# Two-layer backbone on one core: expert weights split 2,048 wide, strided reads in place of strided writes, and mixing's even rows in plain fp32

## The chip, the cores and the metric

The kernel runs on one core of a Trainium2 chip. The metric is the device time of one execution in microseconds (us). Five engines work side by side, each through its own instructions in a fixed order: TensorE (PE; its weight loads are PEld), VectorE (DVE), ScalarE (ACT), GpSimd (POOL) and SyncE (SP), which here only issues DMAs. An instruction waits for what it reads, and a write waits until the buffer's last readers are done. TensorE writes into PSUM, and the others read it from there.

## The reference

Two layers over 1,024 tokens of width 1,024, all in fp32. Layer 0 mixes tokens by grouped-query attention, layer 1 by a 2-D Fourier transform in four channel groups followed by a linear map. After each comes a mixture of 32 experts in four groups: top-1 group, then the top two experts in it.

```python
for i in range(DEPTH):                       # DEPTH = 2
    ...
    h = _modulate(x, norm_mix[i], sh1, sc1)  # RMS norm * (1 + scale) + shift
    y = _gqa_attention(...) if kind == 0 else _fourier_mix(h, fourier_w_o[j])
    x = x + g1 * y
    x = x + g2 * _hier_moe(_modulate(x, norm_ffn[i], sh2, sc2), *moe_p)
return _rms_norm(x, final_norm)

def _fourier_mix(h, w_o):
    hg = h.reshape(b, n, FOURIER_GROUPS, d // FOURIER_GROUPS)
    f = jnp.fft.fft2(hg, axes=(1, 3), norm='ortho').real
    return f.reshape(b, n, d) @ w_o

def expert_block(args):                      # per expert: D 1,024, width 512
    xblk, e = args
    return (jax.nn.silu(xblk @ w1[e]) * (xblk @ w3[e])) @ w2[e]
```

## The kernel before

**Products.** A large fp32 product is three products in fp32r, TensorE's faster reading of fp32: each operand is the sum of a high part (a copy rounded to fp32r, by ScalarE) and a low part (the operand minus its high part, mostly by VectorE). mm3 (L207 to L209) multiplies high by high, low weights by high, high by low. wh and wl are the parts of a weight, xh and xl those of an expert's transposed input, gh and gl those of its transposed hidden rows.

**Experts.** phase_moe runs 32 experts on up to 104 gathered rows each. Weights come from memory in 1 MB pieces of 128 by 2,048, two each for w1, w3 and w2. In the order of use they are w1 of expert e, w2 of expert e−1, w3 of e. `quarter` (L1245) takes 1,024 columns of a piece, copies them into wh (L1249) and subtracts into wl (L1254); of every twelfth quarter GpSimd subtracts. There are five pairs of buffers (NSP), and `get` splits three quarters ahead of use (AHEAD). The first five low parts of a layer (NLATE) are put off until after the first gather (`finish_late`, L1264). The next piece is loaded when a raw buffer becomes free (`feed`, L1240). Some pieces lie as a list of two tiles of 1,024.

For expert e the program's order is: w1's first half into h1; gT of expert e−1, four transposes of its hidden rows (L1358), then gh on ScalarE (L1361) and gl on VectorE (L1362); w1's second half; xin of expert e+1, eight transposes of its gathered rows (L1329), then xh (L1330) and xl (L1331); the products with w2 into py; w3 into h3, with `store` of expert e−1 between (y, L1371, and a scatter-add by GpSimd, L1372); `hidden`, which is silu (L1347) and gg = silu(h1) × h3 (L1350). A scheduler then sets each engine's order from its own estimate of times. gT and xin share the PSUM tile pt, one bank of 2 KB per partition, with two buffers. The rows of an expert and their gates come from one-hot products (slot_index: L1202 on VectorE, L1205 on TensorE), four experts at a time.

**Columns.** w1 and w3 lie in memory so that the product's columns come in another order than w2's rows. gg therefore reads its inputs in order and writes at steps of 512 bytes. In the router, `route_half` (L981) does the same for the input of the logits, which route_transpose (L996, L1009) then transposes.

**Routing.** `route_part(g, m, t0, t1)` (L1093 to L1160) turns the logits of a range of 128-token tiles into chosen experts, slots and gates by many small VectorE operations. In layer 1 ROUTE_F cuts the eight tiles in 0 to 4, 4 to 6 and 6 to 8.

**Mixing.** In layer 1 `combine` scales the rows (u, L1724), folds columns c and 256−c into a sum and a difference (L1693), adds rows i and i+512 with their norms into ef (even) and subtracts them for the odd ones (L1743, L1762). `parts` splits ef into eh and el (L1700, L1701) and multiplies both by a table in high and low parts (U and UE). From the second pair on, GpSimd does a part of u, the difference folds and a running sum S of ef. `transform` then splits U (L1815) and goes on, `project` writes the mixed rows.

Of the kernel before, what the change touches and what calls it, by code (L numbers as in the profile page):

```python
# [56 lines left out]
ROUTE_F = ((0, 4), (4, 6), (6, 8))  # L57
# [4 lines left out]
AHEAD = 3  # L62
NSP = 5
NSP_EARLY = 3
# [3 lines left out]
NLATE, POOL_LAST = 5, 380  # L68
# [23 lines left out]
def host_tables():  # L92
# [28 lines left out]
    for k, v in (("pc", pc), ("ps", ps), ("cc", cc), ("cs", cs)):  # L121
        r[f"dft_{k}h"], r[f"dft_{k}l"] = two_parts(v)
# [822 lines left out]
def route_setup(g, mo, one, wk):  # L945
# [9 lines left out]
    r.gain = lambda: nc.vector.scalar_tensor_tensor(r.A2, r.A2, 1.0, nf, OP.add, OP.mult)  # L955
# [236 lines left out]
def slot_index(g, m, wk, pp, n, posm, val, tag):  # L1192
# [4 lines left out]
    for e in range(n):  # L1197
        oh = wk.tile([P, NT, CAP], BF, name="oneh", bufs=3)
# [16 lines left out]
class Moe:  # L1215
# [28 lines left out]
    def quarter(self, t, i):  # L1244

        nc = self.g.nc
        t = t[i] if isinstance(t, list) else t[:, i * 1024:(i + 1) * 1024]
        h, l = (self.hp.tile([P, 1024], F32R, name=n) for n in ("wh", "wl"))
        nc.scalar.copy(h, t)  # L1249
        if self.ns < NLATE:  # L1250
            self.late.append((l, t, h))
            return h, l
        pool = self.ns > 11 and self.ns % 12 == 9 and (self.ns < POOL_LAST or not self.l)
        i = (nc.gpsimd if pool else nc.vector).tensor_sub(l, t, h)  # L1254
        if pool:
            self.sub = i.ins
        else:
            self.vsub = i.ins
        return h, l

    def finish_late(self):

        for l, t, h in self.late:
            self.vsub = self.g.nc.vector.tensor_sub(l, t, h).ins  # L1264
# [37 lines left out]
    def get(self, n):  # L1302
        self.split(n + AHEAD)
        return self.sp.pop(n)
# [833 lines left out]
```

## Time and profile before

| | us |
|---|---|
| median of 3 runs | 2320.17 |
| lowest and highest | 2315.22, 2320.39 |
| the profiled execution | 2314.98 |
| its span in the trace | 2313.2 |

| engine | busy us | share of the span | instructions |
|---|---|---|---|
| PE | 2107.3 | 91% | 10250 |
| DVE | 1935.2 | 84% | 2822 |
| ACT | 1339.3 | 58% | 1741 |
| POOL | 1070.3 | 46% | 560 |

The span runs from the first to the last instruction; the execution has some 2 us around it. The granted clock of TensorE is 0.957 of full speed on average. In a row of the trace the first number is the start or a total in us; "out<-in" names the tiles; an arrow in brackets tells how long the engine was idle before and what ended that. Matmuls follow each other closer than their own durations, so their rate is read from the distance of starts.

### The profile page before, as it was taken

To read this page: it belongs to the slowest core of one execution; us is meant where nothing else is said; L and a number is where in the kernel's file an instruction comes from. 1 tells how busy PE (TensorE), PEld (TensorE's weight loads), DVE (VectorE), ACT (ScalarE), POOL (GpSimd) and SP (SyncE) were. 2 spreads that over 40 slices of the span, in tenths; PEclk is the share of its full clock that TensorE was granted. 3 is DMA by queue.
4 is the path that set the end of the run, shared out by engine and by line. 5 is a ranking of instruction groups with operands and counts; after the bars stand their busy time and mean duration, and the time that the engine had idled before them with its cause. 6 is when DMAs were issued, how large, how long until landed. Compare 5 with 4: busy or idle time off the path is not lost. (4 is left out here: it accounts for less than half of the span.)

```text
span 2313.2 us, 29541 instructions
## 1 busy us (share of the span) xinstructions
PE 2107.3 (91%) x10250; PEld 1436.2 (62%) x10250; DVE 1935.2 (84%) x2822; ACT 1339.3 (58%) x1741; POOL 1070.3 (46%) x560
## 2 busy tenths in 40 slices
PE   6899899999999869999999999589699999999993
PEld 3677444545446647677776776357476777777662
DVE  4878566666668789999999999666899999999995
ACT  4743444444443237677776777343487777776774
POOL 2322677777777623344334443533233444434433
PEclk8999899999999879999999999789799999999997
DMA  8544534534335779999999999644699989999996
GB/s 305 187 157 150 175 119 135 197 119 133 115 113 189 260 262 318 356 371 314 369 353 336 377 363 339 231 179 168 237 335 350 375 299 368 359 352 342 357 352 204
DMA packets 152630, 614.21 MB, mean 266 GB/s; under 512 B 26961, under 2 KB 43993, under 8 KB 106461
## 3 DMA queue, kind: packets, MB, share of 16 engines
q1 hardware_dynamic: 110188, 546.87, 64.0%
q0 software_dynamic: 24672, 54.40, 9.4%
q10 hardware_dynamic: 17616, 11.01, 1.5%
q8 instruction: 82, 1.34, 0.2%
q14 instruction: 72, 0.58, 0.1%
HBM read 559.57 MB, written 78.44 MB: 276 GB/s over the span
## 5 line engine op out<-in xcount | busy, mean ns | idle before, releaser
L208 PE MATMUL h<-wl,xh 128*104 128x512 f32 x1024 | 410.5, 401 | 18.1 <-DVE wl L1254 18.1
L207 PE MATMUL h<-wh,xh 128*104 128x512 f32 x1024 | 409.8, 400 | 0.0
L209 PE MATMUL h<-wh,xl 128*104 128x512 f32 x1024 | 406.0, 396 | 0.0
L563 DVE TENSOR_REDUCE m<-sm 128x1 f32<-128x512 f32 x360 | 201.8, 593 | 107.6 <-PE sm L562 107.1
L1318 POOL DMA_INDIRECT xg<-H,idx x64 | 116.3, 1818 | 281.4 <-PE pt L1329 126.0
L208 PEld LDWEIGHTS h<-wl,xh 128*104 128x104 f32 x1024 | 173.5, 169 | 89.4 <-DVE wl L1254 29.7
L1372 POOL DMA_INDIRECT Xs<-y,idx x64 | 192.5, 3007 | 76.3 <-DVE y L1371 47.7
L1249 ACT CAST wh<-raw 128x1024 fp32r<-128x1024 f32 x196 | 200.3, 1056 | 33.9 <-PE h L209 21.0
L1254 DVE TENSOR_TENSOR wl<-raw,wh 128x1024 fp32r<-128x1024 f32 x175 | 211.9, 1251 | 6.4 <-ACT wh L1249 6.3
L1254 DVE TENSOR_TENSOR wl<-wl,wh 128x1024 fp32r<-128x1024 f32 x163 | 211.9, 1328 | 1.8 <-ACT wh L1249 1.8
L207 PEld LDWEIGHTS h<-wh,xh 128*104 128x104 f32 x1024 | 173.5, 169 | 60.9 <-ACT xh L1330 0.5
L209 PEld LDWEIGHTS h<-wh,xl 128*104 128x104 f32 x1024 | 173.5, 169 | 60.0
L1254 DVE TENSOR_TENSOR wl<-wh 128x1024 fp32r<-128x1024 f32 x157 | 208.4, 1350 | 2.7 <-ACT wh L1249 2.3
L1249 ACT CAST wh<-wh 128x1024 fp32r<-128x1024 f32 x180 | 186.2, 1054 | 38.5 <-PE h L209 27.2
L208 PE MATMUL py<-wl,gh 128*104 128x512 f32 x512 | 203.9, 399 | 0.2 <-DVE wl L1254 0.2
L209 PE MATMUL py<-wh,gl 128*104 128x512 f32 x512 | 200.9, 394 | 0.3 <-DVE gl L1362 0.3
L1249 ACT CAST wh<-wl 128x1024 fp32r<-128x1024 f32 x172 | 178.3, 1054 | 35.5 <-PE h L209 26.5
L207 PE MATMUL py<-wh,gh 128*104 128x512 f32 x512 | 196.8, 403 | 2.0 <-ACT gh L1361 1.8
L1249 ACT CAST wh<-X 128x1024 fp32r<-128x1024 f32 x124 | 129.6, 1053 | 52.1 <-PE h L209 41.4
L1254 DVE TENSOR_TENSOR wl<-X,wh 128x1024 fp32r<-128x1024 f32 x113 | 141.3, 1282 | 3.9 <-ACT wh L1249 3.8
L1254 POOL TENSOR_TENSOR wl<-wh 128x1024 fp32r<-128x1024 f32 x23 | 68.5, 2977 | 158.7 <-issue 98.9
L562 PE MATMUL sm<-KS,qs 128*128 128x512 f32 x360 | 135.5, 383 | 0.0
(584 smaller groups left out, 4778.7 us busy)
## 6 DMA issues: line engine op xcount, KB each, us to landing
raw<-in_moe_w_dram SPq DMA_DIRECT2D x98, 1024.0 KB
wh<-in_moe_w_dram SPq DMA_DIRECT2D x90, 1024.0 KB
wl<-in_moe_w_dram SPq DMA_DIRECT2D x86, 1024.0 KB
qs<-in_moe_w_dram SPq DMA_DIRECT2D x96, 512.0 KB
raw<-in_w_mod_dram SPq DMA_DIRECT2D x43, 1024.0 KB
X<-in_moe_w_dram SPq DMA_DIRECT2D x37, 1024.0 KB
X<-in_moe_w_dram SPq DMA_DIRECT2D x50, 512.0 KB
QS<-qst ACTq DMA_DIRECT2D x32, 256.0 KB
```

Source lines behind the costliest of these rows:

```text
L207: nc.tensor.matmul(out, lh, wh, start=start, stop=False)
L208: nc.tensor.matmul(out, lh, wl, start=False, stop=False)
L209: nc.tensor.matmul(out, ll, wh, start=False, stop=stop)
L562: nc.tensor.matmul(ps[:, :kn], qs[:, h, qt * P:(qt + 1) * P], g.KS[:, g4, k0:k0 + kn], start=True, stop=True)
L563: nc.vector.reduce_max(m3[:, h, qt, b:b + 1], ps[:, :kn], axis=AX.X)
L1249: nc.scalar.copy(h, t)
L1254: i = (nc.gpsimd if pool else nc.vector).tensor_sub(l, t, h)
L1318: self.last = self.g.nc.gpsimd.indirect_dma_start(out=xg, out_offset=None, in_=self.H if src is None else src, in_offset=bass.IndirectOffs ...
L1372: return y, lambda: nc.gpsimd.indirect_dma_start(out=self.X, out_offset=bass.IndirectOffsetOnAxis(ap=idx, axis=0), in_=y, in_offset=None, ...
```

## The change

Five edits go together. (1) A whole piece (2,048 columns) is split by one copy and one subtraction, in three pairs of buffers; `get` hands out halves of it and splits two pieces ahead of use; three low parts are put off in place of five. Of every sixth piece VectorE does the first 1,024 columns and GpSimd the others. List pieces still take two operations each. (2) pt is one tile of two banks with one buffer, so xin makes xh and xl by one operation each, and gT and xin use the same tile in turn; py is one tile of two banks and y one operation. (3) silu and gg read at steps of 8 bytes in PSUM and write in order; route_half reads at 16-byte steps and writes in order, and `gain` reorders its factor once, by a ScalarE copy. (4) In layer 1 the last two route parts become one, at the end. (5) In combine ef goes into plain fp32 products with one table, without eh, el and S, and VectorE does u and all folds; ScalarE does the two-column copies.

```diff
-ROUTE_F = ((0, 4), (4, 6), (6, 8))
+ROUTE_F = ((0, 4), (4, 8))
 
 
 IB = 4
 GA = 3
-AHEAD = 3
-NSP = 5
-NSP_EARLY = 3
+NSP = 3
+NSP_EARLY = 2
 NRAW = (2, 3)
 NHELD = 11
 DROP1, DROP2 = (10, (3, 4)), (27, 2)
-NLATE, POOL_LAST = 5, 380
+NLATE, POOL_LAST = 3, 190
...
-    for k, v in (("pc", pc), ("ps", ps), ("cc", cc), ("cs", cs)):
+    r["dft_pc"] = pc
...
     nc.gpsimd.tensor_copy(by_weights(r.B2), b2.rearrange("t (q p j) -> t q p j", q=2, j=4))
-    r.gain = lambda: nc.vector.scalar_tensor_tensor(r.A2, r.A2, 1.0, nf, OP.add, OP.mult)
+
+    def gain():
+        nc.vector.scalar_tensor_tensor(nf, r.A2, 1.0, nf, OP.add, OP.mult)
+        nc.scalar.copy(r.A2.rearrange("t (q j p) -> t q j p", q=2, j=4), nf.rearrange("t (q p j) -> t q j p", q=2, j=4))
+
+    r.gain = gain
...
     ns = slice(n * 512, n * 512 + 512)
-    x, a2 = (v[:, ns].rearrange("t (p j) -> t p j", j=4) for v in (x1, r.A2))
-    g.nc.vector.tensor_mul(by_weights(r.u[t])[:, n], x, a2)
+    u, a2 = (v[:, ns].rearrange("t (j p) -> t j p", j=4) for v in (r.u[t], r.A2))
+    g.nc.vector.tensor_mul(u, x1[:, ns].rearrange("t (p j) -> t j p", j=4), a2)
...
-        oh = wk.tile([P, NT, CAP], BF, name="oneh", bufs=3)
+        if e == 2 and n == 3:
+            oh = wk.tile([P, DE], F32, name="gg", bufs=1).bitcast(BF)[:, :NT * CAP].rearrange("p (t c) -> p t c", t=NT)
+        else:
+            oh = wk.tile([P, NT, CAP], BF, name="oneh")
...
-        while self.nl < min((self.ns - len(self.late)) // 2 + self.nraw, self.limit):
+        while self.nl < min(self.ns - len(self.late) + self.nraw, self.limit):
             self.raw[self.nl] = self.load(*self.order[self.nl], eng)
             self.nl += 1
 
-    def quarter(self, t, i):
+    def half(self, t, ns=None):
 
         nc = self.g.nc
-        t = t[i] if isinstance(t, list) else t[:, i * 1024:(i + 1) * 1024]
-        h, l = (self.hp.tile([P, 1024], F32R, name=n) for n in ("wh", "wl"))
-        nc.scalar.copy(h, t)
-        if self.ns < NLATE:
-            self.late.append((l, t, h))
-            return h, l
-        pool = self.ns > 11 and self.ns % 12 == 9 and (self.ns < POOL_LAST or not self.l)
-        i = (nc.gpsimd if pool else nc.vector).tensor_sub(l, t, h)
-        if pool:
-            self.sub = i.ins
+        h, l = (self.hp.tile([P, 2048], F32R, name=n) for n in ("wh", "wl"))
+        pool = ns is not None and ns > 5 and ns % 6 == 4 and (ns < POOL_LAST or not self.l)
+        if isinstance(t, list):
+            todo = [(l[:, c:c + 1024], v, h[:, c:c + 1024], pool and c) for c, v in zip((0, 1024), t)]
+        elif pool:
+            nc.scalar.copy(h, t)
+            todo = [(v[0], v[1], v[2], c) for c in (0, 1024) for v in [[u[:, c:c + 1024] for u in (l, t, h)]]]
         else:
-            self.vsub = i.ins
+            todo = [(l, t, h, 0)]
+        if isinstance(t, list) or not pool:
+            for v in todo:
+                nc.scalar.copy(v[2], v[1])
+        if ns is not None and ns < NLATE:
+            self.late.append(todo)
+        else:
+            self.rest(todo)
         return h, l
 
+    def rest(self, todo):
+        for l, t, h, pool in todo:
+            i = (self.g.nc.gpsimd if pool else self.g.nc.vector).tensor_sub(l, t, h).ins
+            if pool:
+                self.sub = i
+            else:
+                self.vsub = i
...
+    @staticmethod
+    def quarter(t, j):
+        return [v[:, 1024 * j:1024 * j + 1024] for v in t]
...
 
     def split(self, n):
 
-        while self.ns <= min(n, 2 * len(self.order) - 1):
-            i, j = divmod(self.ns, 2)
-            self.sp[self.ns] = self.quarter(self.raw[i], j)
-            if j:
-                del self.raw[i]
+        while self.ns <= min(n, len(self.order) - 1):
+            self.sp[self.ns] = self.half(self.raw.pop(self.ns), self.ns)
             self.ns += 1
             self.feed()
 
     def get(self, n):
-        self.split(n + AHEAD)
-        return self.sp.pop(n)
+
+        i, j = divmod(n, 2)
+        self.split(i + NSP - 1)
+        return self.quarter(self.sp.pop(i) if j else self.sp[i], j)
...
         xl = self.wk.tile([P, KD, CAP], F32R, name="xl")
+        pt = self.ps.tile([P, 2, 512], F32, name="pt")
         for q in range(2):
-            pt = self.ps.tile([P, 4, CAP], F32, name="pt", bufs=2)
             for j in range(4):
-                nc.tensor.transpose(pt[:, j], xg[:, (4 * q + j) * P:(4 * q + j + 1) * P], g.ident[:CAP, :CAP])
-            nc.scalar.copy(xh[:, 4 * q:4 * q + 4], pt)
-            nc.vector.tensor_sub(xl[:, 4 * q:4 * q + 4], pt, xh[:, 4 * q:4 * q + 4])
+                nc.tensor.transpose(pt[:, q, j * CAP:j * CAP + CAP], xg[:, (4 * q + j) * P:(4 * q + j + 1) * P], g.ident[:CAP, :CAP])
+        pt = pt[:, :, :4 * CAP]
+        hv, lv = (t.rearrange("p (q j) n -> p q (j n)", q=2) for t in (xh, xl))
+        nc.scalar.copy(hv, pt)
+        nc.vector.tensor_sub(lv, pt, hv)
         return xh, xl
 
...
     def hidden(self, h1, h3):
         nc = self.g.nc
         s_ = self.wk.tile([CAP, DE], F32, name="s", bufs=1)
-        nc.scalar.activation(s_, h1, AF.Silu)
+
+        h1, h3 = (h.rearrange("t (i p j) -> t i j p", i=2, j=2) for h in (h1, h3))
+        sv = s_.rearrange("t (i j p) -> t i j p", i=2, j=2)
+        nc.scalar.activation(sv, h1, AF.Silu)
         gg = self.wk.tile([P, DE], F32, name="gg", bufs=1)[:CAP]
-
-        nc.vector.tensor_mul(gg.rearrange("t (i j p) -> t i p j", i=2, j=2), s_.rearrange("t (i p j) -> t i p j", i=2, j=2),
-                             h3.rearrange("t (i p j) -> t i p j", i=2, j=2))
+        nc.vector.tensor_mul(gg.rearrange("t (i j p) -> t i j p", i=2, j=2), sv, h3)
...
     def gT(self, gg):
         nc = self.g.nc
-        pt = self.ps.tile([P, 4, CAP], F32, name="pt", bufs=2)
+        pt = self.ps.tile([P, 2, 512], F32, name="pt")[:, 0, :4 * CAP].rearrange("p (j n) -> p j n", j=4)
         for j in range(4):
...
         y = self.wk.tile([CAP, D], F32, name="y")
-        for n in range(2):
-            ns = slice(n * 512, (n + 1) * 512)
-            nc.vector.scalar_tensor_tensor(y[:, ns], py[n], gate, self.G2[:CAP, ns], OP.mult, OP.mult)
+        nc.vector.scalar_tensor_tensor(y, py.rearrange("t n c -> t (n c)"), gate, self.G2[:CAP], OP.mult, OP.mult)
...
-                py = [mo.psum("py", 2) for n in range(2)]
+                py = mo.ps.tile([CAP, 2, 512], F32, name="py")
                 for i in range(4):
                     p = mo.get(k + i)
                     for n in range(2):
-                        mo.mm(py[n], gT, p, i, n, 1)
+                        mo.mm(py[:, n], gT, p, i, n, 1)
...
-            def fold(eng, dst, src, op):
+            def fold(dst, src, op, copy):
                 v = src.rearrange("p (g c) -> p g c", g=4)
-                g.last_fold = eng.tensor_tensor(dst[:, :, 1:128], v[:, :, 1:128], v[:, :, 255:128:-1], op).ins
+                g.last_fold = nc.vector.tensor_tensor(dst[:, :, 1:128], v[:, :, 1:128], v[:, :, 255:128:-1], op).ins
                 if op == OP.add:
-                    eng.tensor_copy(dst[:, :, 0:129:128], v[:, :, 0:129:128])
+                    copy(dst[:, :, 0:129:128], v[:, :, 0:129:128])
...
-                for s_, eng in enumerate((nc.vector, nc.gpsimd if i else nc.vector)):
+                for s_ in range(2):
                     u = one.tile([P, D], F32, name=f"u{s_}")
-                    eng.tensor_mul(u, g.X[:, i + 4 * s_], A1)
+                    nc.vector.tensor_mul(u, g.X[:, i + 4 * s_], A1)
                     add = wk.tile([P, 4, 129], F32, name=f"add{s_}")
                     with g.tc.issue_after(after[0]) if after and s_ else nullcontext():
-                        fold(nc.vector, add, u, OP.add)
-                    fold(nc.gpsimd, sub[2 * (i % 2) + s_], u, OP.subtract)
+                        fold(add, u, OP.add, nc.scalar.copy)
+                    fold(sub[2 * (i % 2) + s_], u, OP.subtract, None)
...
-                ef = (wk if i else one).tile([P, 4, 129], F32, name="ef" if i else "ef0")
+                ef = wk.tile([P, 4, 129], F32, name="ef")
                 ief = nc.vector.scalar_tensor_tensor(ef, add[1], r1, add[0], OP.mult, OP.add).ins
-                eh, el = parts_of(ef, wk, "e")
-                after = ief, self.split
-                nc.scalar.activation(dif[0], dif[0], AF.Copy, scale=r0)
                 last = i == 3
                 for q in range(4):
...
+                    nc.tensor.matmul(U[q], ef[:, q, 0:P], pc[:, i], start=False, stop=last)
+                nc.tensor.matmul(UE, ef[:, :, 128], pc[:, i], start=False, stop=last)
+                if i == 0:
+                    nc.tensor.matmul(U5, ef[:, 0, 0:P], zero.bitcast(F32), start=True, stop=False)
+                nc.tensor.matmul(U5[0:4, 8:10], ef[:, :, 128], alt, start=False, stop=False)
+                for q in range(4):
+                    nc.tensor.matmul(U5[:, 2 * q:2 * q + 2], ef[:, q, 0:P], alt, start=False, stop=last and q == 3)
+                after = ief, nc.scalar.activation(dif[0], dif[0], AF.Copy, scale=r0).ins
                 ov, o1 = (v.rearrange("p g c -> p (g c)") for v in dif)
                 nc.vector.scalar_tensor_tensor(ov, o1, r1, ov, OP.mult, OP.subtract)
                 nc.scalar.copy(OQ[0][:, i], ov)
...
@@ -1955,14 +1972,13 @@
             self.st.close()
             mo.open_vectors()
             mo.open_weights()
-            route_part(g, mo.m, *ROUTE_F[1])
             route_transpose(g, r, 3, rwk, pt_)
             route_transpose(g, r, 7, rwk, pt_)
             mo.begin_weights(r)
             route_logits(g, r, 3, rwk, pt_)
             with g.tc.issue_after(g.lt):
                 mo.split(NSP - 1)
-            route_part(g, mo.m, *ROUTE_F[2])
+            route_part(g, mo.m, *ROUTE_F[1])
```

In the rows below, each name carries the number of its tile; the place is expert 20 of layer 0. VectorE before, from gg of expert 19 on, where gl is the hidden rows' low part and wl_11342 a quarter of w1, wl_11356 and wl_11375 the first quarters of w2:

```order
L1350 TENSOR_TENSOR gg_11335<-s_11333,h3_11286 104x2x128x2
L1254 TENSOR_TENSOR wl_11342<-qs_11069,wh_11341 128x1024
L1362 TENSOR_TENSOR gl_11371<-pt_11365,gh_11370 128x416
L1254 TENSOR_TENSOR wl_11356<-wh_11095,wh_11355 128x1024
L1254 TENSOR_TENSOR wl_11375<-wh_11095,wh_11374 128x1024
L1331 TENSOR_TENSOR xl_11397<-pt_11398,xh_11396 128x416
L1331 TENSOR_TENSOR xl_11397<-pt_11405,xh_11396 128x416
```

VectorE after, at the same place; wl_10786 and wl_10812 are the two halves of w2:

```order
L1377 TENSOR_TENSOR gg_10779<-s_10777,h3_10733 104x512
L1275 TENSOR_TENSOR wl_10786<-X_2551,wh_10785 128x2048
L1275 TENSOR_TENSOR wl_10812<-wh_10566,wh_10811 128x2048
L1388 TENSOR_TENSOR gl_10808<-pt_10802,gh_10807 128x416
L1275 TENSOR_TENSOR wl_10847<-wl_10639,wh_10846 128x2048
L1356 TENSOR_TENSOR xl_10830<-pt_10831,xh_10829 128x832
```

Before, one quarter of w1 stands between gg and gl, and all of w2 behind gl; after, both halves of w2 stand there, and xl is one operation behind half of w3.

ScalarE before, from the last copy of w1 on (gh and xh are high parts):

```order
L1249 CAST wh_11341<-qs_11069 128x1024
L1361 CAST gh_11370<-pt_11365 128x416
L1249 CAST wh_11355<-wh_11095 128x1024
L1249 CAST wh_11374<-wh_11095 128x1024
L1330 CAST xh_11396<-pt_11398 128x416
L1330 CAST xh_11396<-pt_11405 128x416
```

ScalarE after:

```order
L1266 CAST wh_10785<-X_2551 128x2048
L1266 CAST wh_10811<-wh_10566 128x2048
L1387 CAST gh_10807<-pt_10802 128x416
L1266 CAST wh_10846<-wl_10639 128x2048
L1375 ACTIVATE s_10922<-h1_10784 104x512
L1355 CAST xh_10829<-pt_10831 128x832
```

The copies of both halves of w2 stand ahead of gh now, and a half of w3 ahead of silu and xh.

TensorE before, at the end of w1's products (h1), with the transposes of the gathered rows (xg) into pt:

```order
L208 MATMUL h1_11340<-wl_11342,xh_11221 104x512
L209 MATMUL h1_11340<-wh_11341,xl_11222 104x512
L1329 MATMUL pt_11398<-ident_83,xg_7345 128x104 x4
L1329 MATMUL pt_11405<-ident_83,xg_7345 128x104 x4
L207 MATMUL py_11415<-wh_11355,gh_11370 104x512
L208 MATMUL py_11415<-wl_11356,gh_11370 104x512
L209 MATMUL py_11415<-wh_11355,gl_11371 104x512
```

TensorE after:

```order
L208 MATMUL h1_10784<-wl_10756,xh_10680 104x512
L209 MATMUL h1_10784<-wh_10755,xl_10681 104x512
L207 MATMUL py_10845<-wh_10785,gh_10807 104x512
L208 MATMUL py_10845<-wl_10786,gh_10807 104x512
L1352 MATMUL pt_10831<-ident_82,xg_7338 128x104 x8
L209 MATMUL py_10845<-wh_10785,gl_10808 104x512
```

The eight transposes moved behind the first two products with w2, just ahead of the first one that reads gl, and they write one tile, that of gT.

## Rows read from the trace of the kernel before

**Rows 1.** Windows: us, busy PE, PEld, DVE, ACT, POOL, clock, DMA share, GB/s.

```profile
966.00:1451.50 485.50, 475.85 (x2346) 347.06 (x2345) 471.06 (x477) 357.96 (x414) 199.47 (x76) 1.00 0.98 354
1765.00:2252.00 487.00, 473.78 (x2332) 345.77 (x2332) 476.30 (x483) 360.05 (x414) 196.81 (x76) 1.00 0.98 352
...
2082.30:2085.70 3.40, 3.40 (x12) 2.40 (x11) 3.40 (x4) 0.11 (x1) 3.17 (x1) 0.50 0.93 381
```

**Rows 2.** Line L1358 on TensorE in each plateau: ns min/median/max, first to last start.

```profile
L1358 PE MATMUL pt<-ident,gg x108: 250/253/309, 966.0 to 1451.8; 104*128 104x104 f32 x108
...
L1358 PE MATMUL pt<-ident,gg x108: 250/253/378, 1765.2 to 2252.7; 104*128 104x104 f32 x108
```

**Rows 3.** Timeline of TensorE: start us, us, instruction.

```profile
1105.49 0.40 PE L207 MATMUL h<-wh,xh 128*104 128x512 f32 x1
...
1113.60 0.39 PE L209 MATMUL h<-wh,xl 128*104 128x512 f32 x1
...
1270.36 0.88 PE L1329 MATMUL pt<-ident,xg 104*128 104x104 f32 x8
```

**Rows 4.** Groups of TensorE, whole span: busy us, mean ns | idle before.

```profile
L1205 PE MATMUL pi<-val,oneh 128*104 128x5 bf16 x512 | 33.8, 193 | 8.0 <-DVE oneh L1202 7.7
```

**Rows 5.** Lines L201 and L202, 2,048 wide: ns min/median/max.

```profile
L201 ACT CAST wh<-raw x8: 1892/1910/1917, 29.7 to 711.4; 128x2048 fp32r<-128x2048 f32 x8
...
L202 DVE TENSOR_TENSOR wl<-raw,wh x8: 2228/2292/4185, 32.0 to 714.4; 128x2048 fp32r<-128x2048 f32 x8
```

**Rows 6.** Timeline of expert 14, layer 0.

```profile
1150.92 3.48 DVE L1254 TENSOR_TENSOR wl<-raw,wh 128x1024 fp32r<-128x1024 f32 x3
...
1154.95 0.58 PE L1329 MATMUL pt<-ident,xg 104*128 104x104 f32 x4 [1.23 <-DVE gl L1362]
```

**Rows 7.** Groups of VectorE by shape (L1933: window 1400 to 1700 alone).

```profile
L1371 DVE SCALAR_TENSOR_TENSOR y<-py,gate,G 104x512 f32<-104x512 f32 x128 | 90.1, 742 | 3.4 <-PE py L209 3.4
...
L1350 DVE TENSOR_TENSOR gg<-s,h 104x512 f32<-104x512 f32 x64 | 69.3, 1082 | 5.1 <-PE h L209 4.8
...
L1933 DVE TENSOR_TENSOR X<-X,mm 128x512 f32<-128x512 f32 x6 | 4.1, 686 | 0.0
...
L981 DVE TENSOR_TENSOR h<-X,A 128x512 f32<-128x512 f32 x32 | 44.2, 1417 | 4.6 <-DMA H<-h 3.3 <-POOL X L1936 1.0
```

**Rows 8.** Timeline of VectorE in layer 1's routing.

```profile
1649.01 0.22 DVE L1153 TENSOR_TENSOR aoh<-aoh,boh 128x64 f32<-128x64 f32 x1
...
1649.56 0.23 DVE L1155 TENSOR_TENSOR aoh<-aoh,val 128x64 f32<-128x64 f32 x1
```

**Rows 9.** Timeline of expert 20, layer 0.

```profile
1268.70 0.51 ACT L1361 CAST gh<-pt 128x416 fp32r<-128x416 f32 x1 [4.39 <-PE pt L1358]
...
1269.24 0.59 DVE L1362 TENSOR_TENSOR gl<-pt,gh 128x416 fp32r<-128x416 f32 x1 [0.47 <-ACT gh L1361]
```

**Rows 10.** Timeline of VectorE and GpSimd, two low parts at once.

```profile
1108.31 2.41 POOL L1254 TENSOR_TENSOR wl<-X,wh 128x1024 fp32r<-128x1024 f32 x1 [6.68 <-issue]
...
1109.55 2.25 DVE L1254 TENSOR_TENSOR wl<-qs,wh 128x1024 fp32r<-128x1024 f32 x1 [0.23 <-ACT wh L1249]
```

**Rows 11.** Window of combine, columns as in rows 1.

```profile
1489.70:1532.90 43.20, 23.21 (x69) 14.39 (x68) 42.18 (x62) 21.90 (x39) 28.57 (x16) 0.70 0.57 222
```

**Rows 12.** Groups of VectorE in that window.

```profile
L157 DVE TENSOR_TENSOR fsta<-fsta,fstv 128x2 f32<-128x2 f32 x4 | 4.9, 1222 | 0.0
...
L1701 DVE TENSOR_TENSOR el<-ef,eh 128x516 fp32r<-128x516 f32 x4 | 3.7, 923 | 0.1
...
L155 DVE RECIPROCAL frs<-fsta 128x2 f32<-128x2 f32 x4 | 0.6, 152 | 0.0
```

**Rows 13.** Timeline: plain fp32 products in attention, the first split of transform.

```profile
599.73 1.94 PE L666 MATMUL po<-wl,V 128*64 128x512 f32 x8
...
1535.20 1.07 ACT L1815 CAST raw<-u 128x512 fp32r<-128x512 f32 x2 [3.99 <-PE ue L208]
```

**Rows 14.** Timeline of TensorE in layer 1, ahead of the last window of rows 1.

```profile
2080.95 0.48 PE L208 MATMUL h<-wl,xh 128*104 128x512 f32 x1 [1.80 <-DVE wl L1254]
```

More of the change, by code (lines that the diff above doesn't have):

```diff
@@ L120, in host_tables @@
          "dft_msk": (m[:, None] > 0)}
-    for k, v in (("pc", pc), ("ps", ps), ("cc", cc), ("cs", cs)):
+    r["dft_pc"] = pc
+    for k, v in (("ps", ps), ("cc", cc), ("cs", cs)):
         r[f"dft_{k}h"], r[f"dft_{k}l"] = two_parts(v)
@@ L1238, in feed @@
     def feed(self, eng=None):
[L1240 removed]
+        while self.nl < min(self.ns - len(self.late) + self.nraw, self.limit):
             self.raw[self.nl] = self.load(*self.order[self.nl], eng)
             self.nl += 1
[L1244 removed]
+    def half(self, t, ns=None):
         nc = self.g.nc
[L1247 to L1259 removed]
+        h, l = (self.hp.tile([P, 2048], F32R, name=n) for n in ("wh", "wl"))
[5 more added lines that the diff above has]
+            todo = [(v[0], v[1], v[2], c) for c in (0, 1024) for v in [[u[:, c:c + 1024] for u in (l, t, h)]]]
+        else:
+            todo = [(l, t, h, 0)]
[6 more added lines that the diff above has]
+            self.rest(todo)
+        return h, l
+    def rest(self, todo):
[8 more added lines that the diff above has]
+        return [v[:, 1024 * j:1024 * j + 1024] for v in t]
     def finish_late(self):
[L1263 to L1264 removed]
+        for todo in self.late:
+            self.rest(todo)
         self.late = []
@@ L1516, in phase_moe @@
             if e and not late:
-                py = [mo.psum("py", 2) for n in range(2)]
+                py = mo.ps.tile([CAP, 2, 512], F32, name="py")
                 for i in range(4):
@@ L1520, in phase_moe @@
                     for n in range(2):
-                        mo.mm(py[n], gT, p, i, n, 1)
+                        mo.mm(py[:, n], gT, p, i, n, 1)
                 k += 4
@@ L1594, in phase_moe @@
                 for i in range(2):
-                    t = mo.load(which, bass.ds(re, 1), i)
+                    t = mo.half(mo.load(which, bass.ds(re, 1), i))
                     for j in range(2):
@@ L1598, in phase_moe @@
             gT = mo.gT(mo.hidden(*hs))
-            py = [mo.psum("py", 2) for n in range(2)]
+            py = mo.ps.tile([CAP, 2, 512], F32, name="py")
             for i in range(2):
-                t = mo.load(2, bass.ds(re, 1), i)
+                t = mo.half(mo.load(2, bass.ds(re, 1), i))
                 for j in range(2):
@@ L1604, in phase_moe @@
                     for n in range(2):
-                        mo.mm(py[n], gT, w, 2 * i + j, n, 1)
+                        mo.mm(py[:, n], gT, w, 2 * i + j, n, 1)
             mo.store(py, idx, gate)[1]()
@@ L1642, in __init__ @@
         fa = self.fa = g.pool(self.sA, "foA", 1, side="right")
-        self.pc = [dft_table(g, g.raw, "pc" + w, "raw") for w in "hl"]
+        self.pc = dft_table(g, g.raw, "pc", "raw").bitcast(F32)
         g.tc.add_manual_dep(g.table, mo.vsub.name,
@@ L1705, in combine @@
             bs = one.tile([1, 4, 129], F32, name="bs")
-            fold(nc.vector, bs, self.B1, OP.add)
+            fold(bs, self.B1, OP.add, nc.vector.tensor_copy)
             bs = parts_of(bs, one, "bs")
@@ L2078 @@
     g.tab = {}
-    for n in ("pch", "pcl", "psh", "psl", "cch", "ccl", "csh", "csl", "c0", "ce", "ci", "ca", "alt"):
+    for n in ("pc", "psh", "psl", "cch", "ccl", "csh", "csl", "c0", "ce", "ci", "ca", "alt"):
         g.tab[n] = dram.tile(list(a["dft_" + n].shape), F32, name="tab_" + n)
```

14 lines of the change are left out of this document (1 added, 13 removed).

## The prediction

> **What bounds the kernel now.** I read the tenths by slice first, then busy time by window, because the change touches almost only the experts and the experts fill more than half of the span. In the two plateaus (after each layer's first experts) TensorE is busy 475.9 of 485.5 us and 473.8 of 487.0, VectorE 471.1 and 476.3, and the DMA engines are at 0.98; ScalarE is busy three quarters of the time and GpSimd two fifths, and the granted clock is 1.00 [rows 1]. So three engines are near their limit at once, and an operation saved on one pays only as far as the others let it. Next I measured the step: the transposes of gT mark each expert, and 108 of them are 27 groups of four. From the first group to the last are 485.8 us in layer 0 and 487.5 in layer 1, over 26 steps 18.67 and 18.74 us per expert [rows 2].
>
> What would an expert take if TensorE never waited? 35 intervals from 1105.49 to 1113.60 give 0.232 us per product [rows 3]. An expert has 72 products and twelve 104-wide transposes, eight of them 0.88 us in a row [rows 3] and four of gT at the same rate, so 72 × 0.232 + 12 × 0.089 = 17.75. The slot products, 33.8 us over 64 experts [rows 4], add at most 0.53: 18.28, call it 18.25. The plateaus therefore lose only about 0.4 to 0.5 us per expert to waits. That is all that narrower work on VectorE could give back there, some 11 + 13 = 24 us.
>
> **Halves in place of quarters: work.** VectorE's 2,048-wide subtraction, used elsewhere in the kernel, has a median of 2.29 us and a minimum of 2.23; ScalarE's copy 1.91 [rows 5]. Three quarters in a row take 3.48 us [rows 6], 2.32 for two. A pair merged saves about 0.04, and I take 0.04 for merged y (0.742 each, [rows 7]) and xl (two of 416 wide in one) too. Seven merged pairs are 0.3 us per expert. gg's 1.08 us [rows 7] holds a write at 512-byte steps; a contiguous 512-wide operation takes 0.686 [rows 7], so 0.40 more goes if reading at steps costs nothing. VectorE gets 0.7 us per expert.
>
> A row close to this: VectorE reads at 10-byte steps in 0.23 where the contiguous neighbour takes 0.22 [rows 8]. No row reads PSUM at 8-byte steps, as silu and gg now do. Bounds: nothing, or the 0.4 lost as before; I take nothing, the nearest row. The Trainium skill (SBUF — State Buffer, Door 1: The DMA port swizzle) says that an access which crosses to a new line each time pays, with lines of 16 bytes in SBUF and 8 in PSUM. By it gg would stay at its old 1.08, and route_half's reads at 16-byte steps would pay too; the row with 10-byte steps does not show such a price, and no row here has the PSUM case.
>
> **Halves: what is queued ahead of whom.** Before, xin's transposes need only the PSUM bank that is two back, and at most two quarters usually stand ahead of gl. In expert 20 gh starts at 1268.70, gl at 1269.24, and the transposes at 1270.36 wait for nothing [rows 3, 9]. Where three subtractions in a row run ahead of gl (expert 14, at 1150.92), the second four transposes start at 1154.95 and TensorE loses 1.23 us [rows 6]. In the changed order the late form is the rule: both 2,048-wide halves of w2 stand ahead of gl in 23 of the 27 plateau experts of layer 0 and 21 of 27 in layer 1, and ScalarE copies the second of them ahead of gh. Its buffer is the one that w1's first half is being read from, since there are only three.
>
> Count from that half's first product, T = 0. A half is twelve products, 2.78; gT's transposes end at 3.14. The buffer is free when its last product ends, 2.94 (a product's record lasts 0.40, [rows 3]). The copy runs from 2.98 to 4.89, then gh (0.51, [rows 9]) to 5.39; the subtraction from 4.94 to 7.22, then gl (0.59, [rows 9]) to 7.81. TensorE does w1's second half until 5.92 and two products of w2 until 6.38; then comes the third, which reads gl, and ahead of it the eight transposes, which now need the one pt tile and so gl as well. TensorE waits for 7.85, that is 1.47 us. What is late next: xh and xl have ample time behind it (products of w2 follow, 24 × 0.232 = 5.6). gg's successor, the second half of w1, meets GpSimd: a 2.41 us subtraction there stretches VectorE's neighbour from 1.2 to 2.25 [rows 6, 10]. In one expert of two GpSimd takes a quarter, so up to 0.4 us on average; I take the middle, 0.18.
>
> Steps with this wait: 17.75 + 1.47 + 0.18 = 19.40 (slot products fill the wait where they occur); the other experts 18.25. Layer 0: 23 × 19.40 + 4 × 18.25 = 519.2 against 27 × 18.67 = 504.1, +15. Layer 1: 21 × 19.40 + 6 × 18.25 = 516.9 against 506.0, +11. Together +26. Low end: no GpSimd wait, copy and subtraction at their minimum (−0.08): 19.14 gives +9 and +5, so +14. High end: slot products lie outside the wait, 19.93 gives +27 and +22, so +49.
>
> **Starts of the layers.** The first four experts of a layer have no late form and are bound by VectorE alone, which still holds the slots of the next experts. Four experts × 0.7 us save 3 per layer (0 to 6). Three halves are put off where five quarters were: 6.9 instead of 5.8 us, +1 per layer. Sum −4.
>
> **Mixing.** In combine VectorE is busy 42.2 of 43.2 us [rows 11]. Of this, two-column operations that read what GpSimd shares with it are stretched: L157's take 1.22 us on average where L155's take 0.15 [rows 12]. There are six such groups of four; together they cost 18.6, at 0.15 each they would cost 3.6. With GpSimd out of it, that excess of 15 falls away, el (3.7, [rows 12]) goes, and three u of 1,024 (twice 0.686) and eight folds (0.686) come over, 9.6: 42 falls to about 33. TensorE pays: a plain fp32 product costs 0.9 us (eight records of four such products, two side by side, in 1.94 [rows 13]) against three of 0.232, so 20 × 0.2 = +4 at full clock. The window's clock is 0.70 [rows 11], so the products alone may take 20 × 0.9 / 0.7 = 26 from the first ef at about 1500. I let the first transform copy, which starts at 1535.20 [rows 13], start at 1529.5: −6. Bounds: −9, if VectorE alone decides; +4, if TensorE at half clock does.
>
> **Routing.** route_half writes at steps in 1.42 us on average, 32 times [rows 7]; at 0.686 it saves 0.7, most of it beside transposes that wait on DMA or X. I take −4 over two layers; −12 if all the layer-1 half counts, +2 if strided reads cost as the writes did and only the added ScalarE copy remains. Layer 1's middle part (35 operations like the two of [rows 8]) now runs merged with the last one: 35 times about 0.2 us fall away, each merged one grows by 0.06, so −5 at best; but work that could fill gaps now stands behind the last logits, +1 at worst. I take −2. None of these is hidden work, since the experts can't start before the slots.
>
> **Sum.** +26 − 4 − 6 − 4 − 2 = +10 to the profiled execution's 2314.98 (span 2313.2): 2325. The median of the three runs, 2320.17, lies 5 above that execution, and the runs reach from 2315.22 to 2320.39, so I forecast 2330.
>
> **Rivals.** Changes within 7 us (0.3%, 2313 to 2327) can't be told from none here.
> *The wait does not come* (faster). Speaks for it: VectorE has 0.7 us more room per expert, seven fewer starts, and it was as full as TensorE. If it drains its queue earlier, gl comes before the second half of w2 is due, and the wait shrinks to what GpSimd causes: 18.25 + 0.18 = 18.43 gives 27 × (0.24 + 0.31) = −15, with the −16 of the other terms −31: 2289. With no wait at all 2280, with half of the other terms 2297. Against it: the copy can't start before the buffer is free, and this time is TensorE's own.
> *The wait comes at its low end* (same). +14 with −16, or −36 to +6 for the others at all their bounds: mostly 2313 to 2326, at the centre 2318. DMA at 0.98 speaks for it: it lets neither side move far.
> *The clock falls* (slower still). After 1.80 us without work at 2080.95 the clock stood at 0.50 for 3.4 us, at a cost of 1.7, while expert 14's wait of 1.23 stands in a plateau of mean 1.00 [rows 1, 6, 14]. The new wait of 1.47 to 1.65 lies between the two. If half of the 44 late experts lost 1.7, that is +37: 2367.
> *Strided PSUM reads cost what the strided write did* (slower still). gg stays at 1.08, 0.4 later in each late expert, and so is the low half behind it: 44 × 0.4 = +18, 2348. This is the rule of the Trainium skill named above (SBUF — State Buffer, Door 1: The DMA port swizzle).
>
> **Chances.** Main case 0.37, clock 0.05, strided PSUM reads 0.05: slower 0.47. Low end: same 0.20. No wait: faster 0.33. The main case's own range is 2327 to 2345. The range that should hold 8 in 10 runs from 2291 to 2352: it cuts the lower third of the no-wait case (0.11), the clock case (0.05) and the upper half of the strided one (0.02).
>
> **What would show it.** Right: in the plateaus the transposes of xin have gl as their releaser, with 1.2 to 1.7 us, in most experts; the gT marks stand 19 to 19.5 us apart; VectorE's busy share falls to about 0.9; gg takes 0.7. In combine the first transform copy comes about 6 us earlier after combine's start, and two-column operations take 0.15. Wrong: gT marks under 18.5 us apart, or gl starting before TensorE has finished w1's second half; then the count above misplaced the second w2 half, and rival one holds. gg at 1.1 or clock below 0.97 in the plateaus would mean one of the last two rivals.

## The result, and the profile after

The changed kernel takes 2336.9 us (median of 4 runs, 2333.1 to 2338.1) against 2317.7; the ratio is 1.0087, with a 95% interval of 1.0074 to 1.0100. The forecast was 2330 with a range of 2291 to 2352. So the kernel got slower by 19 us in the medians where the forecast had added +10; of its cases the main one, with a chance of 0.37, came. The profiled execution has a span of 2334.6 us, 21.4 more than before.

Where the 21.4 us lie is read from gT of expert 0 and of expert 4, 30 and 31 in each layer, as differences of the two traces: up to gT of expert 0 in layer 0 +4.4; experts 0 to 4 −0.2; layer 0's plateau +9.2; its last step −0.3; from there to gT of expert 0 in layer 1 −4.0; experts 0 to 4 +0.7; layer 1's plateau +6.8; the last step and the end +2.0 and +2.8.

The plateaus after, with the windows set to the same marks (columns as in [rows 1]):

```profile
970.30:1465.00 494.70, 477.35 (x2345) 346.31 (x2345) 444.10 (x310) 343.08 (x250) 229.18 (x76) 1.00 0.97 346
1774.90:2268.90 494.00, 475.31 (x2332) 344.32 (x2332) 445.50 (x330) 345.29 (x269) 221.32 (x75) 1.00 0.98 349
```

VectorE has 27 and 31 us less to do than in [rows 1], 444.1 and 445.5 us, and TensorE about the same (1.5 us more), yet each plateau is longer. The marks of gT themselves, which stood 18.67 and 18.74 apart [rows 2]:

```profile
L1384 PE MATMUL pt<-ident,gg x108: 251/253/310, 970.3 to 1465.3; 104*128 104x104 f32 x108
...
L1384 PE MATMUL pt<-ident,gg x108: 250/253/436, 1774.9 to 2269.5; 104*128 104x104 f32 x108
```

494.7 and 494.0 us over 26 steps are 19.03 and 19.00 us per expert. The usual step is 19.22; some experts have 17.83. One usual expert of layer 0, in order of time:

```profile
1256.00 2.28 DVE L1275 TENSOR_TENSOR wl<-wl,wh 128x2048 fp32r<-128x2048 f32 x1
1256.13 0.58 PE L1384 MATMUL pt<-ident,gg 104*128 104x104 f32 x4
1256.27 1.91 ACT L1266 CAST wh<-wh 128x2048 fp32r<-128x2048 f32 x1 [0.89 <-PE h L209]
...
1258.08 0.50 ACT L1387 CAST gh<-pt 128x416 fp32r<-128x416 f32 x1
1258.21 2.29 DVE L1275 TENSOR_TENSOR wl<-wh 128x2048 fp32r<-128x2048 f32 x1
...
1260.42 0.58 DVE L1388 TENSOR_TENSOR gl<-pt,gh 128x416 fp32r<-128x416 f32 x1
1261.06 0.93 PE L1352 MATMUL pt<-ident,xg 104*128 104x104 f32 x8 [1.12 <-DVE gl L1388]
```

This is the chain that the prediction counted. The copy of w2's second half starts at 1256.27, when w1's first half has been read; gh follows it on ScalarE; VectorE subtracts both halves of w2 first; gl comes last, and TensorE has been idle for 1.12 us when it does. In expert 20 of the kernel before, gl was done before the transposes were due [rows 3, 9]. Over the whole span, the view of the tile pt on TensorE says what the transposes into it waited for, gT's and xin's (us, times):

```profile
L1352 PE MATMUL pt<-ident,xg x512: 250/253/433, 867.0 to 2255.3; 104*128 104x104 f32 x171
...
  DVE gl L1388: 32.4, 41
```

41 waits, 32.4 us as the trace puts them down. Before, gl held these transposes for 2.5 us in all. In 16 of the 41, sixteen slot products stand in the wait, as the prediction said they would, and only 0.34 to 0.55 us of idle time is left; the step is some 19.2 us there too:

```profile
1108.67 0.89 PE L1213 MATMUL pi<-val,oneh 128*104 128x5 bf16 x16
1109.93 0.93 PE L1352 MATMUL pt<-ident,xg 104*128 104x104 f32 x8 [0.37 <-DVE gl L1388]
```

The operations that were to become shorter, to be set against [rows 7] (gg, route_half, y) and against two of 0.58 (xl):

```profile
L1395 DVE SCALAR_TENSOR_TENSOR y<-py,gate,G 104x1024 f32<-104x1024 f32 x64 | 81.7, 1277 | 8.6 <-PE py L209 8.6
L1356 DVE TENSOR_TENSOR xl<-pt,xh 128x832 fp32r<-128x832 f32 x64 | 65.0, 1016 | 0.3 <-ACT xh L1355 0.3
...
L986 DVE TENSOR_TENSOR h<-X,A 128x512 f32<-128x512 f32 x32 | 44.8, 1420 | 5.0 <-DMA H<-h 3.8 <-POOL X L1953 1.0
L1377 DVE TENSOR_TENSOR gg<-s,h 104x512 f32<-104x512 f32 x64 | 43.2, 675 | 0.0
```

gg fell from 1.08 to 0.675, what a contiguous operation takes; route_half did not move, 1.42 before and after. In combine, from its first u to the first split of transform:

```profile
1501.40:1537.90 36.50, 27.61 (x83) 13.24 (x82) 29.16 (x61) 20.27 (x44) 1.36 (x2) 0.73 0.77 294
```

```profile
L1767 DVE SCALAR_TENSOR_TENSOR ef<-add,frs,add 128x516 f32<-128x516 f32 x4 | 3.0, 742 | 3.5 <-PE u L1776 3.5
...
L157 DVE TENSOR_TENSOR fsta<-fsta,fstv 128x2 f32<-128x2 f32 x4 | 0.6, 148 | 0.0
```

```profile
1537.85 0.58 ACT L1832 CAST raw<-u 128x512 fp32r<-128x512 f32 x1 [3.94 <-PE u L1770]
1538.71 0.58 ACT L1832 CAST raw<-u 128x512 fp32r<-128x512 f32 x1 [0.27 <-PE u L1770]
```

With GpSimd out of it, two-column operations like L157's take 0.148 instead of 1.22 us [rows 12], VectorE needs 29.2 instead of 42.2 [rows 11], and now the last ef waits for TensorE (3.5 us): at the end the plain fp32 products set the pace. The last four end 0.86 us apart, and each split waits for its own. From layer 0's last gT to the first split are 58.6 us instead of 69.1, so 10.5 less; at the first logits 6.8 of it are left, since the splits come at TensorE's pace. Part of such a difference is spread between traces: from layer 0's last gT to combine's first u the runs below take 18.8 to 24.4 us. From that u to the first split all traces agree: 45.5 to 47.3 us in the three with the old mixing, 35.2 to 36.8 in the eleven with the new one.

### The profile page after: what moved, and what is told of

Read it like the earlier page. It is cut to its first block, busy times and chain, and to the rows that moved or that the text cites. A ratio compares the mean times of both kernels' runs of the same rounds, so it can differ in the third digit from the quotient of the medians.

```text
span 2334.6 us, 28475 instructions
## 1 busy us (share of the span) xinstructions
PE 2119.3 (91%) x10255; PEld 1433.7 (61%) x10255; DVE 1865.1 (80%) x2392; ACT 1298.5 (56%) x1367; POOL 1093.5 (47%) x546
## 5 line engine op out<-in xcount | busy, mean ns | idle before, releaser
L1341 POOL DMA_INDIRECT xg<-H,idx x64 | 143.0, 2234 | 348.8 <-PE pt L1352 258.1
L1275 DVE TENSOR_TENSOR wl<-raw,wh 128x2048 fp32r<-128x2048 f32 (+1 forms) x97 | 212.9, 2200 | 47.2 <-ACT wh L1266 36.7
L1275 DVE TENSOR_TENSOR wl<-wh 128x2048 fp32r<-128x2048 f32 (+1 forms) x90 | 209.9, 2333 | 31.8 <-ACT wh L1266 24.9
L1266 ACT CAST wh<-raw 128x2048 fp32r<-128x2048 f32 x82 | 156.1, 1905 | 84.7 <-PE h L209 50.3
L1275 DVE TENSOR_TENSOR wl<-wl,wh 128x2048 fp32r<-128x2048 f32 (+1 forms) x85 | 186.3, 2192 | 18.3 <-ACT wh L1266 11.6
L1266 ACT CAST wh<-wh 128x2048 fp32r<-128x2048 f32 x81 | 154.5, 1907 | 71.4 <-PE h L209 50.2
L1266 ACT CAST wh<-wl 128x2048 fp32r<-128x2048 f32 x69 | 131.5, 1906 | 66.0 <-PE h L209 51.0
L1275 DVE TENSOR_TENSOR wl<-X,wh 128x1024 fp32r<-128x1024 f32 (+1 forms) x90 | 143.3, 1613 | 17.8 <-ACT wh L1266 9.8
L1266 ACT CAST wh<-X 128x1024 fp32r<-128x1024 f32 (+1 forms) x82 | 110.0, 1365 | 56.3 <-PE h L209 35.8
L660 PE MATMUL st<-qs,KS 128*128 128x512 f32 x320 | 129.6, 405 | 0.0
```

The source lines that it names most:

```text
L660: nc.tensor.matmul(ps[:, h], g.KS[:, g4, ks], qs[:, h], start=True, stop=False)
L1266: nc.scalar.copy(v[2], v[1])
L1275: i = (self.g.nc.gpsimd if pool else self.g.nc.vector).tensor_sub(l, t, h).ins
L1341: self.last = self.g.nc.gpsimd.indirect_dma_start(out=xg, out_offset=None, in_=self.H if src is None else src, in_offset=bass.IndirectOffs ...
```

## The experiments

Ratios are to the kernel before on the same chip, with 95% intervals; the changed kernel's is 1.0087.

**a1_gl_first.**

```diff
+                if e and not late:
+                    with tc.issue_after(mo.gl_i):          # w2's second half: its low part behind gl
+                        mo.split((k + 2) // 2 + NSP - 1)
+                    mo.dcp = mo.cp
...
-        nc.scalar.activation(sv, h1, AF.Silu)
+        with self.g.tc.issue_after(self.dcp) if self.dcp else nullcontext():
+            nc.scalar.activation(sv, h1, AF.Silu)
```

> The changed kernel with one edge more: the low part of w2's second half is issued behind gl on VectorE, and silu behind that half's copy on ScalarE; by the order this takes one of the two halves from ahead of gl in about 26 of the 44 late plateau experts. Theory 1 (gl waits behind two low halves, and TensorE for gl): in those experts the step falls from 19.2 to 18.0 to 18.3 us, the others stay at 19.2; total 2337 - 26 = 2311 (2306 to 2316). Rival A (the DMA engines at 0.97 bind): no run of steps falls below 18.7; total 2320 or more. Rival B (three buffers bind, so the half moved back is late for its own products): TensorE's wait moves to the products with w2's low part, steps stay near 19; total 2332 to 2338.

Measured: 2313.1, ratio 0.9973 (0.9962 to 0.9984), 24 us under the changed kernel in the medians and 26 by the ratios. Both halves stand ahead of gl in 19 plateau experts instead of 44. Plateaus 483.5 and 481.8. The transposes' waits by releaser:

```profile
  DVE gg L1379: 14.1, 12
...
  DVE gl L1390: 0.8, 2
```

The wait for gl is all but gone, and the total fell by about what theory 1 gave, for the two order rules together; 7.7 us came back as longer waits for gg (6.4 in the changed kernel). Steps of 17.8 stand three in a row, so rival A is out for so short a stretch; the plateaus' mean is 18.5 to 18.6.

**a3_pt_banks.** pt as before, in two tiles of one bank, with xh and xl in two operations each; halves and all else as in the change. The scheduler's order moves with it: both halves of w2 stand ahead of gl in 37 plateau experts, not 44.

```diff
-        pt = self.ps.tile([P, 2, 512], F32, name="pt")
         for q in range(2):
+            pt = self.ps.tile([P, 4, CAP], F32, name="pt", bufs=2)
```

> The changed kernel with pt as before: two rotating tiles of one bank, xh and xl in two operations each. Theory 1: half of xin's transposes no longer wait for gl, so 0.4 us per late expert leave the wait, 44 x 0.4 = 18: 2319 (2316 to 2324). Rival: the third product with w2 waits for gl anyway and the tile costs nothing: 2334 to 2339.

Measured: 2310.2, ratio 0.9961 (0.9946 to 0.9976), 27 us under the changed kernel (29 by the ratios), more than the 18 expected; plateaus 482.8 and 486.0. The view of its tile pt:

```profile
  DVE gl L1386: 6.4, 10
```

Of the 32.4 us of waits for gl 26 are gone. The two plateaus are shorter by 20 us; the rest of the gain lies in the starts and the end.

**c_quarters.** The weights in quarters again; pt one tile, and all else as in the change.

```diff
-NSP = 3
+AHEAD = 3
+NSP = 5
...
-    def half(self, t, ns=None):
+    def quarter(self, t, i):
```

> The changed kernel with the weights split in quarters of 1,024 in five buffers as before (AHEAD 3, five late low parts); all other edits stay. Theory 1 (the halves cause the plateaus' and the starts' loss): plateaus at 18.3 to 18.7 us per expert, starts 6 us shorter, total 2301 to 2315. Rival (the shared pt tile or the merged operations cause it): plateaus stay at 19.0, total 2328 to 2338.

Measured: 2310.5, ratio 0.9963 (0.9951 to 0.9975). Plateaus 484.8 and 485.8, the way from layer 0's last gT to layer 1's first 211.1 instead of 217.2, last step and end 62.7 instead of 65.7. The transposes wait for gl 13 times, 5.2 us. Halves with two pt tiles (a3) and quarters with one (c) are both 27 us faster than halves with one (29 by the ratios): it takes both to make the loss. Theory 1 had the total and the plateaus right; but neither theory's wording, that one of them is the cause, was.

**e1_gl_and_pt and e2_gl_pt_old_router.** The edits of a1 and a3 together; in e2 the two hunks on route_half and gain are undone besides.

> The changed kernel with both edits, that of a1_gl_first and that of a3_pt_banks. Theory 1 (what is left of the wait for gl in either goes): plateaus from 483 to about 476 us, total 2300 to 2306. Rival (in either alone the plateaus already stand at what VectorE's queue allows, where one-hot groups of 4 us and gg come late): plateaus 481 to 484, total 2308 to 2313.

> As e1_gl_and_pt, with the router's edit undone (route_half writes at steps, gain as before). Theory 1 (the router's edit saves nothing, and its cost in b3_router is within the noise): within 3 us of e1_gl_and_pt. Rival (the edit costs or saves what it was sized at, 4): 4 us or more apart.

Measured: e1 2305.9, ratio 0.9946 (0.9933 to 0.9959); e2 2302.1, 0.9935 (0.9923 to 0.9947). The total of e1 is at theory 1's upper end, but its plateaus (483.8 and 481.2) are the rival's: the transposes' waits for gl are down to 1.0 us, from 6.4 in a3 and 0.8 in a1, and nothing came of it there. e2 is faster than e1 by 3.8 us in the medians and 2.5 by the ratios, with overlapping intervals: between theory 1 and the rival, and not settled.

**a4_fewer_loads.** The test of what holds the plateaus at 481 to 486.

```diff
-            self.raw[self.nl] = self.load(*self.order[self.nl], eng)
+            if w == 1 and i and 4 <= x < 31:
+                self.raw[self.nl] = self.kept
```

> The changed kernel with two rotating one-bank pt tiles (as in a3_pt_banks), where in experts 4 to 30 of each layer the second half of w3 is not loaded and the first half is used in its place (other results; one of six loads left out). Theory 1 (with the wait for gl gone, the plateaus stand at the rate of the DMA engines, 0.99 busy at 18.55 to 18.7 us per expert, whatever the order): steps fall to 17.8 to 18.3, total 2290 to 2300. Rival (buffers and the order of VectorE bind): steps stay at 18.5 to 18.7, total 2306 to 2312.

Measured: 2322.1, ratio 1.0024 (1.0014 to 1.0034): slower than a3, and neither theory. The window of its plateau in layer 0, and its wait for gl:

```profile
966.90:1455.50 488.60, 477.48 (x2342) 345.24 (x2341) 445.44 (x334) 342.88 (x276) 218.63 (x75) 1.00 0.87 294
```

```profile
  DVE gl L1390: 16.2, 24
```

The DMA engines are at 0.87 and steps are 18.8, so they did not hold this kernel. But the scheduler, which saw other loads, set another order (both halves ahead of gl in 43 plateau experts, 37 in a3) with 16.2 us of waits for gl, so the run does not tell whether they hold a3 or e1. The trace of e1 says more: in its plateaus ScalarE's weight copies waited for a load 3 times, 2.7 us in all, in layer 0 and never in layer 1; 210 of their 230 waits of over 0.15 us were for TensorE's last product from the buffer, and they ended within 0.1 us of that product. So the loads were on time although the DMA engines were at 0.99, and it is TensorE's own work that leaves little room: 26 steps of 18.28, the prediction's count with slot products, are an estimated 475 us, 6 to 9 under e1's plateaus. No run took load off and kept the order.

**b1_mixing, b2_strided_gg, d_mix_strided.** The kernel before with the hunks on mixing alone (b1), with silu, gg, y and py alone (b2), and with both (d).

> The kernel before with the mixing edits alone (even rows in plain fp32, no splits of ef and no running sum, all folds and u on VectorE). Theory 1 (VectorE leads combine, and GpSimd's share of its work slowed it): combine to first logits 6 to 7 us shorter, as between the two traces: ratio 0.997, about 2313. Rival (the gain in the changed kernel came from its later start, or the slower plain fp32 products take it back): 2318 to 2321.

> The kernel before with silu and gg reading PSUM at 8-byte steps and y in one operation (py one tile); quarters, pt, router and mixing as before. VectorE has 0.5 us less work per expert. Theory 1 (TensorE, the DMA engines and the order of the queues hold the plateaus, not VectorE's sum, as c_quarters' plateaus of 485 us say): 2314 to 2319. Rival (VectorE at 0.97 binds): 54 x 0.5 less, 2291 to 2300.

> The kernel before with the mixing edits and those of b2_strided_gg. Theory 1 (the two add up: -4 of b1_mixing and about nothing): 2310 to 2315. Rival (route parts and xin merged are what made c_quarters 9 us faster than before, so that without them less is left): 2315 to 2318.

Measured: b1 2314.1, ratio 0.9981 (0.9970 to 0.9992), 4.4 us by the ratio, theory 1; b2 2307.1, 0.9957 (0.9945 to 0.9970), 10 us; d 2300.6, 0.9933 (0.9920 to 0.9946), 15.5 us, about the sum of the two. b2 lies between both theories, and so d was expected too high: half a microsecond less on VectorE per expert does pay, about a third of what it would if VectorE alone bound. d, with quarters, two pt tiles and the old router, is the fastest of all, level with e2 and some 36 us under the changed kernel. c_quarters differs from it by the one pt tile with merged xh and xl, the merged route parts and the router's edit, and is 7 us slower by the ratios.

**b3_router.**

```diff
-    g.nc.vector.tensor_mul(by_weights(r.u[t])[:, n], x, a2)
+    g.nc.vector.tensor_mul(u, x1[:, ns].rearrange("t (p j) -> t j p", j=4), a2)
```

> The kernel before with the router edit alone (route_half reads at 16-byte steps and writes in order; gain reorders its factor by a ScalarE copy). Theory 1 (a read at 16-byte steps in SBUF costs what the write at steps did, 1.05 us instead of 0.68, so nothing is saved and the copy and another order of layer 0's routing are added): 2319 to 2324. Rival, the step of the forecast (reads at steps are free): 2315 or less, and 0.7 us per operation in the trace.

Measured: 2319.0, ratio 1.0007 (0.9998 to 1.0016): theory 1.

```profile
840.85 1.07 DVE L986 TENSOR_TENSOR h<-X,A 128x512 f32<-128x512 f32 x1
```

One that nothing disturbs takes 1.07 us; before it took 1.03 to 1.10.

**a2_tail and a5_pool_last.** Two tries at the late end. In the changed kernel the last gh waits behind a square of the final norm, and a scatter-add stands behind a late low part of GpSimd.

```diff
-                    fin.tiles(mo.wk)
+                    with tc.issue_after(mo.gh_i):
+                        fin.tiles(mo.wk)
...
-NLATE, POOL_LAST = 3, 190
+NLATE, POOL_LAST = 3, 184
```

> The changed kernel with the squares of the final norm issued behind the last expert's gh on ScalarE. Theory: the 6.3 us that TensorE waits for gh of the last expert come from a square that waits for its rows by DMA ahead of gh; the wait goes and the total falls by 4 to 5, to 2332. Rival: the final norm's chain is the end in either order and only gets later; total stays at 2337.

> The changed kernel with POOL_LAST 184 in place of 190: the last low part that GpSimd makes in layer 1 is one turn (six halves) earlier. Theory 1 (the end is late because expert 29's and 30's scatter-adds stand on GpSimd's queue behind a low part that waits 12.7 us for its copy, and the rows of the final norm come from them): the scatter-adds start some 10 us earlier, the total falls by 4 to 5 from the changed kernel's 2337. Rival (the last scatter-add waits for y of expert 30, which is as late as before): 2336 to 2339.

Measured: a2 2339.8, ratio 1.0090 (1.0072 to 1.0108); a5 2336.1, 1.0080 (1.0066 to 1.0094): both rivals. In a2 gh comes at once, and the squares still start when the rows arrive:

```profile
2290.81 0.51 ACT L1387 CAST gh<-pt 128x416 fp32r<-128x416 f32 x1 [3.60 <-PE pt L1384]
2295.39 1.06 ACT L2020 ACTIVATE raw<-X 128x1024 bf16<-128x1024 f32 x1 [4.08 <-DMA X<-Xs]
```

In a5 the scatter-add no longer has a low part ahead of it, and waits for y instead:

```profile
2266.96 3.37 POOL L1396 DMA_INDIRECT Xs<-y,idx  x1 [16.44 <-DVE y L1395]
2285.09 5.57 POOL L1396 DMA_INDIRECT Xs<-y,idx  x1 [14.76 <-DVE y L1395]
```

So the rows come from y of expert 30, which stands on VectorE behind the low parts of the next half. In the changed kernel these are late because the copies are:

```profile
2278.34 2.29 DVE L1275 TENSOR_TENSOR wl<-raw,wh 128x2048 fp32r<-128x2048 f32 x1 [6.75 <-ACT wh L1266]
```

What makes these copies late is not settled by a run of its own, but three buffers of a half are not enough to do it: from layer 1's second last gT to the end the kernel before takes 60.9 us, the changed one 65.7 and c_quarters 62.7, while a3, e1 and e2, with halves in three buffers and two pt tiles, take 62.5, 61.2 and 60.7. In these traces the late end goes with the wait for gl (a4, with 16.2 us of such waits, 67.5; a1 63.4).

## Why the prediction was right, and where it was off

*The wait for gl* was right in its place, its chain and its size. Measured from that half's first product, as the prediction counted (1253.27): gh done at 5.3 (5.39 forecast), gl at 7.7 (7.81), the transposes at 7.8 (7.85), and 1.12 us of idle time where 1.47 was counted. gl is a little early because each instruction of VectorE starts up to 0.08 before the record of the one ahead ends. The rest is on TensorE: it was 0.13 later with w1's second half, and the trace counts idle time from the end of a product's record (0.40), the prediction from the next product's turn (0.23). In the step the wait costs 19.22 − 17.83 = 1.39. 41 such waits stand where 44 were counted. a1 and a3 take away the wait by two different edits and get the time back, and c by a third, so it is shown.

*The plateaus* came to +16 over 26 steps, +18 with the 27th that the forecast also counted, where +26 was forecast; the term was mis-sized. The 0.18 us per expert for GpSimd's low part beside VectorE's did not come: no product in the plateaus waited for a low part of w1, and the step with the wait is 19.22, which is 17.75 + 1.47, and not 19.40. That is 8 us over 44 experts. The experts without the wait mostly take 17.8 to 18.1, not 18.25.

*The saved work* was sized right for gg (0.675; forecast 0.686) and too small for the rest: by the plateaus' busy time VectorE has 1.0 and 1.2 us less per expert, not 0.7. b2 says what gg and y are worth alone: 10 us. In the changed kernel the saving is lost behind the wait: VectorE is idle for 51 us of layer 0's plateau, 14 before.

*The starts* were forecast at −4 and are some +6: from the last slots to gT of expert 0 layer 0 takes 2.0 and layer 1 3.3 us longer, experts 0 to 4 −0.2 and +0.7. The step that failed is "bound by VectorE alone". With all three halves filled, the fourth copy must wait until expert 0's first half is used, and VectorE stands idle:

```profile
1682.56 2.36 DVE L1275 TENSOR_TENSOR wl<-X,wh 128x1024 fp32r<-128x1024 f32 x2 [5.26 <-ACT wh L1266]
```

Five quarters are freed one by one. From layer 1's last slots to gT of expert 0 all eight traces with halves take 31.7 to 32.9 us and all six with quarters 28.9 to 30.3; of the 6 us that c_quarters is shorter up to layer 1's first gT, 1.9 lie there. No run changed the number of buffers alone.

*Mixing* was forecast at −6: between the traces −6.8 to the first logits, and b1 alone gives 4.4 in the total. The first split comes 9 us earlier after combine's first u, the bound for VectorE deciding alone; what follows gives some of it back. *Routing* was forecast at −6 and gave about nothing (b3; layer 1 from the first logits to the last slots −0.5): the bound "+2 if strided reads cost as the writes did" was the true one, and the 10-byte row that I went by [rows 8] was the wrong neighbour: at route_half's price (1.07 instead of 0.68 on 512 columns) its 64 columns would pay an estimated 0.05 us, too little to see in it. Layer 0 up to its slots is 2.4 us longer, but b1's trace is 2.2 later at the first gT with the same order on all four compute engines there, so that much lies in the spread. *The end* (+4.8) was not in the sum at all.

So a right mechanism and errors of opposite sign: the plateaus 10 too large, the other terms together about +1 instead of −16, and the end left out. That the sum came as near as it did is in part luck. Of the rivals, the clock stayed at 1.00 in the plateaus with idle times of up to 1.26 us, and strided PSUM reads cost nothing.

## What to carry to other kernels

The wider operations took work off VectorE, but no run shows a gain from the halves (d with quarters is level with e2), and they doubled the grain of its queue: before merging, write down what small operation stands behind them and who waits for that. Two edits can each be harmless and lose together; here wide low parts made gl late, and a shared PSUM tile made the next transposes wait for it, so undo them one at a time before giving up both. And of a change of five edits the fastest version, d, has one and parts of two others: time each alone.

## What the runs showed of the hardware

Reading PSUM at 8-byte steps was free on VectorE and ScalarE: gg takes 0.675 us as against 0.686 for a contiguous operation of that width, silu 0.593 as against 0.606 before. Reading SBUF at 16-byte steps was not: route_half's 512 columns take 1.07 us. The Trainium skill (SBUF — State Buffer, Door 1: The DMA port swizzle) says that each access which crosses to a new line pays, with lines of 16 bytes in SBUF and 8 in PSUM, and names matmuls as what slows down in PSUM. The row of route_half agrees with it; the row of 10-byte steps, 0.23 us [rows 8], is too small to tell; the rows of gg and silu show no price in PSUM for these two engines, and no run here has a matmul at such steps.

A two-column operation of VectorE takes 0.15 us, and 1.2 on average beside GpSimd's folds [rows 12]; taking GpSimd out shortened VectorE's busy time there from 42.2 to 29.2 us although VectorE took over its three u and eight folds (el, 3.7 us, fell away and the two-column copies went to ScalarE).
